# Binary cross-entropy on one core: two 64 KiB slots with float32 targets and even and odd partitions instead of three 56 KiB slots with bfloat16 targets

## The chip, the core and the metric

The kernel runs on one core of one Trainium2 chip. The metric is the device time of one execution in microseconds. Before the change the median of three runs is 1864.77 us (1864.36 to 1865.55). Data lie in the chip's main memory (HBM). A core has a working memory, SBUF, of 128 partitions; 16 DMA engines move data between the two. DVE (VectorE) and ACT (ScalarE) compute; POOL (GpSimd), SP (SyncE) and ACT each have a queue from which transfers are started.

## The reference

Two float32 arrays of 8192 x 8192 come in, `pred` and `target`; a target is 0 or 1. One array of the same shape goes out:

```
eps = 1e-7
pred = np.clip(pred, eps, 1 - eps)
return -(target * np.log(pred) + (1 - target) * np.log(1 - pred))
```

Each array has 268.4 MB, so at least 536.9 MB are read and 268.4 MB written. As a target is 0 or 1, the result is -log|p + t - 1|, and this is what the kernel computes.

## The kernel before

The arrays are seen flat. A chunk is a stretch of the flat array, laid out as 128 rows, one for each partition, of w columns of float32; a chunk's row is contiguous in HBM. Per partition there are 524288 columns in all. `plan` cuts them into 40 chunks: two of 5120 columns (`FIRST`), 35 of 14336 (`BIG`), two of 5632 (`LAST`; called a and b) and one of 1024 (`TAIL`; c).

Two buffers stay for the whole run. `ring_p` holds predictions, and results in their place: three slots of 56 KiB per partition, filled in turn, and a place for c. `ring_t` has a single slot for targets in bfloat16, and a place for c. The transfer casts the targets from float32 on their way.

A chunk goes through five steps, all in place on `ring_p`: DVE clips (`clip`, L88), DVE adds target minus one (`log`, L94, the only reader of `ring_t`), ACT takes the absolute value (L97) and the logarithm (L98), DVE negates (`back`, L102). A big chunk does its steps in two halves of 7168 columns.

The order on each engine is the order in which the program is written (`manual_schedule`), and an engine waits at an instruction until what it needs is there. Nearly all transfers go through POOL's queue: `load_t` (L75), `load_p` (L72) and `store` (L79). ACT's queue starts only the load of prediction 0, in two transfers, one of the even and one of the odd partitions; SP's queue starts the stores of a, b and c (L79, and `store_rows`, L84).

In the loop over the big chunks POOL starts, for chunk k, the load of target k+1, the store of chunk k and the load of prediction k+2. The target load waits for L94 of chunk k, as there is one slot; the store waits for L102 of chunk k; the prediction load goes into the slot of chunk k-1, whose store was started one round before.

Of the kernel before, what the change touches and what calls it, by code (L numbers as in the profile page):

```python
# [1 line left out]

# [4 lines left out]

EPS = 1e-7

BIG = 14 * 1024  # L10
FIRST = 5 * 1024
LAST = 5632
TAIL = 1024
SLOTS = 3


def plan(total):
    n = (total - 2 * FIRST - 2 * LAST - TAIL) // BIG
    assert n > 4 and total == 2 * FIRST + n * BIG + 2 * LAST + TAIL
    spots = [(FIRST, 0, 0), (FIRST, FIRST, FIRST)]  # L20
    spots += [(BIG, k % SLOTS * BIG, 0) for k in range(1, n + 1)]
    end = (n + 1) % SLOTS * BIG
    spots += [(LAST, end, 0), (LAST, end + LAST, LAST)]
    return spots + [(TAIL, SLOTS * BIG, BIG)]


@with_exitstack
def kernel(
    ctx: ExitStack,
    tc: tile.TileContext,  # L30
    pred: bass.AP,
    target: bass.AP,
    out: bass.AP,
):
    nc = tc.nc
    fp32 = mybir.dt.float32
    bf16 = mybir.dt.bfloat16
    Alu = mybir.AluOpType
    Act = mybir.ActivationFunctionType
    P = nc.NUM_PARTITIONS  # L40

    R, C = pred.shape
    spots = plan(R * C // P)
    n = len(spots)
    widths = [s[0] for s in spots]
    cols = [sum(widths[:k]) for k in range(n)]

    def chunk(ap, k):
        flat = ap.rearrange("r c -> (r c)")
        return flat[cols[k] * P : (cols[k] + widths[k]) * P].rearrange("(p w) -> p w", p=P)  # L50

    pool = ctx.enter_context(tc.tile_pool(name="rings", bufs=1))
    ring_p = pool.tile([P, SLOTS * BIG + TAIL], fp32, name="ring_p", tag="ring_p")
    ring_t = pool.tile([P, BIG + TAIL], bf16, name="ring_t", tag="ring_t")
    warm = pool.tile([1, 8], fp32, name="warm", tag="warm")

    def spot(k, part=(0, 1)):
        w, c, _ = spots[k]
        i, m = part
        return ring_p[:, c + i * w // m : c + (i + 1) * w // m]  # L60

    def spot_t(k, part=(0, 1)):
        w, _, c = spots[k]
        i, m = part
        return ring_t[:, c + i * w // m : c + (i + 1) * w // m]

    def load_p(k):
        if k == 0:
            for rows in (slice(0, P, 2), slice(1, P, 2)):
                nc.scalar.dma_start(out=spot(0)[rows], in_=chunk(pred, 0)[rows])  # L70
        else:
            nc.gpsimd.dma_start(out=spot(k), in_=chunk(pred, k))  # L72

    def load_t(k):
        nc.gpsimd.dma_start(out=spot_t(k), in_=chunk(target, k))  # L75

    def store(k):
        queue = nc.sync if k >= n - 3 else nc.gpsimd
        queue.dma_start(out=chunk(out, k), in_=spot(k))  # L79

    def store_rows(k):
        src, dst = spot(k), chunk(out, k)
        for first, last in ((0, 108), (108, 120), (120, 128)):
            nc.sync.dma_start(out=dst[first:last], in_=src[first:last])  # L84

    def clip(k, *part):
        p = spot(k, *part)
        nc.vector.tensor_scalar(  # L88
            out=p, in0=p, scalar1=EPS, scalar2=1 - EPS, op0=Alu.max, op1=Alu.min
        )  # L90

    def log(k, *part):
        p = spot(k, *part)
        nc.vector.scalar_tensor_tensor(  # L94
            out=p, in0=spot_t(k, *part), scalar=1.0, in1=p, op0=Alu.subtract, op1=Alu.add
        )
        nc.scalar.activation(out=p, in_=p, func=Act.Abs)  # L97
        nc.scalar.activation(out=p, in_=p, func=Act.Ln)  # L98

    def back(k, *part):  # L100
        p = spot(k, *part)
        nc.vector.tensor_scalar(out=p, in0=p, scalar1=-1.0, scalar2=None, op0=Alu.mult)  # L102

    with tc.manual_schedule():
        nc.vector.memset(warm, 1.0)  # L105
        load_t(0)
        load_p(0)
        load_t(1)
        load_p(1)
        load_p(2)  # L110
        nc.scalar.activation(out=warm, in_=warm, func=Act.Ln)  # L111
        for k in (0, 1):
            clip(k)
            log(k)
        load_t(2)
        back(0)
        store(0)
        back(1)
        store(1)
        load_p(3)  # L120
        a, b, c = range(n - 3, n)
        for k in range(2, n - 3):
            for h in (0, 1):
                clip(k, (h, 2))
                log(k, (h, 2))
            if k < n - 4:
                load_t(k + 1)
            else:
                load_t(a)
                load_t(b)  # L130
                load_p(c)
                load_t(c)
                back(k, (0, 2))
                for j in (a, b):
                    clip(j)
            if k < n - 4:
                back(k, (0, 2))
            back(k, (1, 2))
            store(k)
            if k + 2 < n - 3:  # L140
                load_p(k + 2)
            elif k + 2 == n - 3:
                load_p(a)
                load_p(b)
        log(a, (0, 2))
        log(a, (1, 2))
        clip(c)
        log(b, (0, 2))
        back(a, (0, 2))
        log(b, (1, 2))  # L150
        back(a, (1, 2))
        store(a)
        log(c)
        back(b, (0, 2))
        back(b, (1, 2))
        store(b)
        back(c)
        store_rows(c)


# [1 line left out]
_INS = ['pred', 'target']  # L162
_OUTS = [((8192, 8192), 'float32')]


# [23 lines left out]
```

## Time and profile before

| | |
|---|---|
| median of three runs | 1864.77 us |
| span of the profiled execution, first to last instruction | 1863.3 us |
| time of the profiled execution beside its span | not listed on its own; the median of the runs is 1.5 us above the span |
| DVE busy | 1121.6 us (60%) |
| ACT busy | 902.4 us (48%) |
| POOL busy, nearly all of it starting transfers | 178.7 us (10%) |
| HBM read and written | 536.87 and 268.44 MB, 432 GB/s over the span |
| DMA packets in POOL's queue | 16704 |

The page gives the busy time of each engine, 40 slices of the span with the busy share of the engines and of the 16 DMA engines in tenths (9 is 90% or more), the DMA queues, and the chain of work that ended last. A group of instructions is one line of the program on one engine, with its shapes, its count, its busy time in us, the mean duration in ns, and the idle time of the engine before these instructions with what ended it. In the order of time a row gives start, duration, engine, line and operation; what stands in brackets is the idle time before it and what ended it. The trace also has a record of every DMA packet (start, duration, size), and the times at which each of the 16 engines reported its share of a transfer.

### The profile page before, as it was taken

What the parts mean: (1) busy time and instruction counts of PE and PEld (TensorE: products, weight loads), DVE (VectorE), ACT (ScalarE), POOL (GpSimd) and SP (SyncE); (2) the same over time, 40 slices, a digit from 0 to 9 for tenths busy, and PEclk for the clock granted to TensorE, in tenths of its full rate; (3) what the DMA queues carried; (4) which work ended last, traced back from release to release, by engine and by line L of the source; (5) the groups of instructions that cost most, each with busy time, mean ns of one, the idle gap of its engine ahead of it and who ended that gap; (6) DMA issues with size and microseconds to landing.
All of it is one profiled execution on the core that took longest, in us unless ns stands there. A gap on an engine that the chain in (4) does not pass through costs nothing.

```text
span 1863.3 us, 713 instructions
## 1 busy us (share of the span) xinstructions
DVE 1121.6 (60%) x230; ACT 902.4 (48%) x156; POOL 178.7 (10%) x120
## 2 busy tenths in 40 slices
DVE  4666555555666566655555666566655555666565
ACT  4454444455555544444445555544444445555554
POOL 1111101111110011101111110011101111110020
DMA  9999999999999999999999999999999999999999
GB/s 344 348 370 356 355 356 355 355 355 355 357 375 374 374 372 355 355 355 355 355 355 355 359 374 374 375 375 361 355 355 356 356 356 355 356 367 374 374 353 352
DMA packets 17318, 671.15 MB, mean 360 GB/s; under 512 B 1952, under 2 KB 1952, under 8 KB 2336
## 3 DMA queue, kind: packets, MB, share of 16 engines
q0 software_dynamic: 16704, 662.18, 99.0%
q1 hardware_dynamic: 448, 6.29, 0.8%
q10 hardware_dynamic: 160, 2.62, 0.4%
q14 instruction: 6, 0.05, 0.0%
HBM read 536.87 MB, written 268.44 MB: 432 GB/s over the span
## 4 chain that ended last, share of the span: by engine, by line
DMA 60%; issue 35%; ACT 3%; DVE 1%; POOL 0%; POOLq 0%; DVEq 0%; PEldq 0%
DMA ring_t<-in_target_dram 58%; DMA ring_p<-in_pred_dram 2%; ACT ring_p L98 1%; ACT ring_p L97 1%; DVE ring_p L94 1%; DVE ring_p L102 0%; POOL out_dram L79 0%; DVE ring_p L88 0%; POOL ring_t L75 0%; POOLq L75 0%; POOL ring_p L72 0%; POOLq L79 0%; DVEq L94 0%; PEldq L184 0%
## 5 line engine op out<-in xcount | busy, mean ns | idle before, releaser
L97 ACT ACTIVATE ring_p<-ring_p 128x7168 f32<-128x7168 f32 (+3 forms) x77 | 452.0, 5870 | 940.7 <-DVE ring_p L94 940.7
L94 DVE SCALAR_TENSOR_TENSOR ring_p<-ring_t,ring_p 128x7168 f32<-128x7168 bf16 (+3 forms) x77 | 558.2, 7251 | 372.0 <-DMA ring_t<-in_target_dram 370.7
L102 DVE TENSOR_SCALAR ring_p<-ring_p 128x7168 f32<-128x7168 f32 (+3 forms) x77 | 285.4, 3707 | 329.4 <-ACT ring_p L98 329.4
L98 ACT ACTIVATE ring_p<-ring_p 128x7168 f32<-128x7168 f32 (+3 forms) x77 | 452.6, 5877 | 2.4
L88 DVE TENSOR_SCALAR ring_p<-ring_p 128x7168 f32<-128x7168 f32 (+3 forms) x75 | 284.6, 3794 | 24.4 <-DMA ring_p<-in_pred_dram 24.4
L79 POOL DMA_DIRECT2D out_dram<-ring_p x37 | 128.0, 3459 | 584.4 <-DVE ring_p L102 584.2
L75 POOL DMA_DIRECT2D ring_t<-in_target_dram x40 | 29.0, 724 | 1057.2 <-DVE ring_p L94 1056.4
L72 POOL DMA_DIRECT2D ring_p<-in_pred_dram x39 | 21.8, 561 | 2.5 <-issue 2.5
L111 ACT ACT_TABLE_LOAD x1 | 1.3, 1283 | 1.9 <-issue 1.9
L105 DVE MEMSET warm<- 1x8 f32 x1 | 0.1, 65 | 0.8 <-PEq L173 0.8
L111 ACT ACTIVATE warm<-warm 1x8 f32<-1x8 f32 x1 | 0.2, 208 | 0.0
L173 POOL MEMSET const-float32-0.0<- 128x1 f32 x1 | 0.1, 99 | 0.2 <-issue 0.2
L173 POOL MEMSET const-bfloat16-1.0<- 128x1 bf16 x1 | 0.1, 102 | 0.0
L173 POOL MEMSET const-uint8-127<- 128x1 uint8 x1 | 0.1, 100 | 0.0
L173 POOL MEMSET const-float32-1.0<- 128x1 f32 x1 | 0.1, 99 | 0.0
## 6 DMA issues: line engine op xcount, KB each, us to landing
ring_p<-in_pred_dram POOLq DMA_DIRECT2D x35, 7168.0 KB, 44.3
out_dram<-ring_p POOLq DMA_DIRECT2D x35, 7168.0 KB, 31.1
ring_t<-in_target_dram POOLq DMA_DIRECT2D x35, 3584.0 KB, 31.3
ring_p<-in_pred_dram POOLq DMA_DIRECT2D x2, 2816.0 KB, 37.1
out_dram<-ring_p SPq DMA_DIRECT2D x2, 2816.0 KB, 14.6
out_dram<-ring_p POOLq DMA_DIRECT2D x2, 2560.0 KB, 27.9
ring_t<-in_target_dram POOLq DMA_DIRECT2D x2, 1408.0 KB, 26.5
ring_p<-in_pred_dram ACTq DMA_DIRECT2D x2, 1280.0 KB, 10.5
```

The lines of the kernel that those rows point to most:

```text
L72: nc.gpsimd.dma_start(out=spot(k), in_=chunk(pred, k))
L75: nc.gpsimd.dma_start(out=spot_t(k), in_=chunk(target, k))
L79: queue.dma_start(out=chunk(out, k), in_=spot(k))
L88: nc.vector.tensor_scalar(out=p, in0=p, scalar1=EPS, scalar2=1 - EPS, op0=Alu.max, op1=Alu.min)
L94: nc.vector.scalar_tensor_tensor(out=p, in0=spot_t(k, *part), scalar=1.0, in1=p, op0=Alu.subtract, op1=Alu.add)
L97: nc.scalar.activation(out=p, in_=p, func=Act.Abs)
L98: nc.scalar.activation(out=p, in_=p, func=Act.Ln)
L102: nc.vector.tensor_scalar(out=p, in0=p, scalar1=-1.0, scalar2=None, op0=Alu.mult)
L105: nc.vector.memset(warm, 1.0)
L111: nc.scalar.activation(out=warm, in_=warm, func=Act.Ln)
L173: nc = _bacc.Bacc("TRN2", target_bir_lowering=False, num_devices=1)
```

## The change

Chunks, slots, types, split and order change together:

- `BIG` becomes 16384 columns, so that a row of a big chunk has 64 KiB; there are two slots for predictions and results instead of three. `FIRST` becomes 3584 and `LAST` 4096 columns; there are 31 big chunks instead of 35.
- `ring_t` holds float32, so target loads no longer cast.
- Stores and prediction loads of the big chunks are made in two transfers, of the even and of the odd partitions, as are the stores of the two first chunks and the prediction loads of a and b. Target loads stay whole. All stay on POOL's queue, but for the load of prediction 0 (ACT) and the stores of a, b and c (SP), as before. The store of the last big chunk is whole.
- Prediction k+1 now goes into the slot of chunk k-1, and each half of its load waits for the same half of that chunk's store. In the loop POOL starts both halves of store k-1, both halves of prediction load k+1, and target load k+1. The target load waits for the subtractions of chunk k.
- Steps of a big chunk are done in four pieces of 4096 columns instead of two of 7168: DVE's order in a round is four subtractions, four negations, four clips of the next chunk. In the last big chunk, the clips of a and b stand between the negations.

```diff
-BIG = 14 * 1024
-FIRST = 5 * 1024
-LAST = 5632
+BIG = 16 * 1024
+FIRST = 3584
+LAST = 4096
 TAIL = 1024
-SLOTS = 3
+SLOTS = 2
+PIECES = 4
...
-    ring_t = pool.tile([P, BIG + TAIL], bf16, name="ring_t", tag="ring_t")
+    ring_t = pool.tile([P, BIG + TAIL], fp32, name="ring_t", tag="ring_t")
...
+    even, odd = slice(0, P, 2), slice(1, P, 2)
+    every = slice(0, P)
+    bulk = nc.gpsimd
+
+    def load_p(k, rows=every, queue=bulk):
+        queue.dma_start(out=spot(k)[rows], in_=chunk(pred, k)[rows])
...
-    def store(k):
-        queue = nc.sync if k >= n - 3 else nc.gpsimd
-        queue.dma_start(out=chunk(out, k), in_=spot(k))
+    def store(k, rows=every, queue=bulk):
+        queue.dma_start(out=chunk(out, k)[rows], in_=spot(k)[rows])
...
         load_t(2)
-        back(0)
-        store(0)
-        back(1)
-        store(1)
-        load_p(3)
+        for k in (0, 1):
+            back(k)
+        for rows in (even, odd):
+            for k in (0, 1):
+                store(k, rows)
         a, b, c = range(n - 3, n)
-        for k in range(2, n - 3):
-            for h in (0, 1):
-                clip(k, (h, 2))
-                log(k, (h, 2))
-            if k < n - 4:
-                load_t(k + 1)
-            else:
-                load_t(a)
-                load_t(b)
+        m = PIECES
+        for i in range(m):
+            clip(2, (i, m))
+        for k in range(2, a):
+            last = k == a - 1
+            if k > 2:
+                for rows in (even, odd):
+                    store(k - 1, rows)
+            if not last:
+                for rows in (even, odd):
+                    load_p(k + 1, rows)
+            if last:
                 load_p(c)
                 load_t(c)
-                back(k, (0, 2))
+                for rows in (even, odd):
+                    for j in (a, b):
+                        load_p(j, rows)
+            for i in range(m):
+                log(k, (i, m))
+            if last:
                 for j in (a, b):
-                    clip(j)
-            if k < n - 4:
-                back(k, (0, 2))
-            back(k, (1, 2))
-            store(k)
-            if k + 2 < n - 3:
-                load_p(k + 2)
-            elif k + 2 == n - 3:
-                load_p(a)
-                load_p(b)
+                    load_t(j)
+            else:
+                load_t(k + 1)
+            for i in range(m):
+                back(k, (i, m))
+                if last and i in (1, 2):
+                    clip(a + i - 1)
+            if not last:
+                for i in range(m):
+                    clip(k + 1, (i, m))
+        store(a - 1)
+        clip(c)
...
-        clip(c)
         log(b, (0, 2))
         back(a, (0, 2))
         log(b, (1, 2))
         back(a, (1, 2))
-        store(a)
+        store(a, queue=nc.sync)
         log(c)
...
-        store(b)
+        store(b, queue=nc.sync)
```

## The prediction

> **What bounds the kernel now.** I read the page's slices first, then its queues, then the chain and the groups, and last the order of time of one chunk.
>
> ```profile
> DVE 1121.6 (60%) x230; ACT 902.4 (48%) x156; POOL 178.7 (10%) x120
> DMA  9999999999999999999999999999999999999999
> q0 software_dynamic: 16704, 662.18, 99.0%
> DMA 60%; issue 35%; ACT 3%; DVE 1%; POOL 0%; POOLq 0%; DVEq 0%; PEldq 0%
> L94 DVE SCALAR_TENSOR_TENSOR ring_p<-ring_t,ring_p 128x7168 f32<-128x7168 bf16 (+3 forms) x77 | 558.2, 7251 | 372.0 <-DMA ring_t<-in_target_dram 370.7
> ```
>
> The 16 DMA engines are in the top tenth in all 40 slices, and POOL's queue (q0) alone holds them for 99.0% of the span. DVE waits 370.7 us for targets, so the engines are fed by the transfers and not the other way round; the chain, which hops from target load to target load, says the same.
>
> ```profile
> 1652.20 0.53 POOL L75 DMA_DIRECT2D ring_t<-in_target_dram  x1 [29.43 <-DVE ring_p L94]
> 1668.98 3.89 DVE L88 TENSOR_SCALAR ring_p<-ring_p 128x7168 f32<-128x7168 f32 x1
> 1669.36 3.63 POOL L79 DMA_DIRECT2D out_dram<-ring_p  x1 [16.63 <-DVE ring_p L102]
> 1672.98 0.53 POOL L72 DMA_DIRECT2D ring_p<-in_pred_dram  x1
> 1683.60 7.62 DVE L94 SCALAR_TENSOR_TENSOR ring_p<-ring_t,ring_p 128x7168 f32<-128x7168 bf16 x1 [10.73 <-DMA ring_t<-in_target_dram]
> 1702.98 0.53 POOL L75 DMA_DIRECT2D ring_t<-in_target_dram  x1 [29.47 <-DVE ring_p L94]
> ```
>
> One chunk of 14336 columns (a column is one float32 on 128 partitions). From the target load at 129.28 to that at 1753.73 there are 32 periods: 50.76 us each, 3.541 ns a column. A period reads 7.34 MB of predictions and 7.34 MB of targets and writes 7.34 MB: 434 GB/s. The page's 360 GB/s counts targets as they arrive, in two bytes. A load issue takes POOL 0.53 us, but 3.63 us where it begins inside a clip on DVE: POOL is held until the clip ends.
>
> The trace's packet records give the limit. On each engine one packet is one partition's row, and the next begins 2113 ns later for 57344 B, 833 ns for 22528 B, 155 ns for 4096 B: 27.2 B/ns plus 4.8 ns a packet. A target packet (57344 B read, 28672 B written in bfloat16) begins 2112 ns after the last: the read side sets its time, and the cast saves none. From 2.85 to 1859.7 us there is no moment in which the engines run dry.
>
> The sum of before: 524288 columns x 3.541 ns = 1856.5 us; 2.1 us pass before the first packet, 1.3 us after the last one (1861.96), and 3.4 us are slow packets at the start and the lag of one engine, which lands its share of a transfer 1.0 us behind the first engine at 45 us and 3.0 us behind from 500 us on. Together 1863.3, the profiled span. The median of the runs is 1864.77, so 1.5 us lie around the span.
>
> **The change part by part.**
> *Float32 targets, 64 KiB rows.* The same bytes are read and written in HBM. A chunk is now 16384 columns; 24 packets per engine at 65536/27.2 + 4.8 = 2414 ns are 57.94 us. Today 24 packets at 2113 ns are 50.71 of the 50.76 us, so three handovers between transfers cost 0.05 us, 0.017 each; five handovers (both halves of store and prediction load, and the target) cost 0.09. 31 chunks x 58.03 = 1798.9 against 35 x 50.76 = 1776.7; the small pieces lose 6144 columns, x 3 x 4 B x 8 rows / 27.2 = 21.7 us. The transfers together change by 1798.9 - 1776.7 - 21.7 = +0.5 us. Fewer packets and more handovers cancel.
>
> *Two slots instead of three.* A prediction load now waits for the store of the chunk two before it, which today it does not. Count from the landing of target k (0), on the engine that is last. The queue then holds store k-1: even half to 9.7 us (4 packets of 2.414), odd half to 19.3; then prediction k+1, even to 29.0, odd to 38.6, and target k+1 to 58.0. Each must be issued before the queue is dry:
> - Even load: its store half lands at 9.7 + 0.3 (at 63 us a last packet ended 0.3 us before its landing). From issue to first packet ACT's first load took 1.3 us (0.74 to 2.07); POOL's first took at most 4.6 (1.24 to 5.82, behind ACT's packets). First data at 11.3 to 14.6, needed at 19.3. DVE is then in the subtractions, beside which no issue of POOL is seen; if they hold it as the clip did, 3.6 us more, up to 18.2. Still covered, by 1.1 to 8 us; I take no hold and 1.3.
> - Behind this wait on POOL stand the odd load and the target load. The odd one is free at 19.6, may be held 2.3 us by a negation (4096 columns between the 1.62 us of 2816 and the 3.10 of 5632), and has data by 26.5; needed at 29.0. The target needs the four subtractions: 4 x 4.42 us (4096 columns between 3.09 at 2816 and 5.49 at 5120) = 17.7; needed at 38.6.
> - Store k needs the last negation: 4.42 + 4 pieces x 2 x 3.61 on ACT (between 2.55 at 2816 and 4.47 at 5120) + 2.29 = 35.6; needed at 58.0. Clips of k+1 end at 38.9 + 4 x 2.29 = 48.1; needed at 58.0.
>
> So nothing per chunk. A float32 second operand of the subtraction isn't in the trace: between 4.42 us (as bfloat16) and twice that. Even doubled, the four end at 35.4, store k is ready near 45, and DVE is busy 54 of 58 us; I take 4.42, since this operation runs at 1.04 ns a column where one-input ones run at 0.52, so it isn't fed by the width of one operand.
>
> *Start.* 15.7 MB are queued before the first wait, to 38.3 us. Prediction 1 lands near 19.6, target 2 can be issued at about 28. The four half stores of chunks 0 and 1 run from 57.6 to 66.0; the even load of chunk 3 is free at 62.1, with data at 63.4 to 66.7, or 70.3 if held: 0 to 4 us once. I take 0.
>
> *End.* Count from the landing of target 32: store 31 to 19.3, chunk c to 21.7, predictions a, b to 31.4, their targets to 41.1. Store 32 waits for negations between which stand the clips of a and b, each waiting for its odd half: a's at 29.3, then clip, negation, clip, negation, 4 x 2.29 = 38.5; data at 39.8 to 43.1, needed at 41.1. 0 to 2 us once; I take 0. After that the stores of 32, a, b, c are issued well before the queue ends, as today.
>
> Sum: 1863.3 + 0.5 = 1863.8, and with the 1.5 around it 1865.3 us.
>
> **Rivals.**
> - *The refill runs dry* (the other side: slower). If the even load's data come later than 9.7 us after its store half ends, every chunk idles by the excess, about 30 times. For it: a landing, a wait and an issue of POOL now lie in the loop. Against: 1.1 to 8 us of margin. At 0.3 us past the margin 1865 + 10 = 1875; at 2 us, 1925. 0.09. [...]
> - *Rows in step.* At 59 us the last packets of a target load took 2280 to 3064 ns instead of 2131, on all 16 engines together; 55 such packets are in the records, most in the first 420 us, until the engines have drifted apart. Rows 64 KiB apart may collide anew in each transfer: one round of 0.5 us in each of 5 x 31 transfers is +78, 1943 us. Against: 4 KiB rows run at the fitted 155 ns, and 0.4% of the packets are slow today. 0.07. [...]
> - *Half transfers don't use all engines from POOL's queue.* Stores and prediction loads, two thirds of 1856 us, would double: 3100 us. Against: ACT's two 64-row loads, with target 0 beside them, moved 5.24 MB between 2.07 and 14.96 us, 407 GB/s with the start-up in it. 0.03.
> - *A 65536 B row goes as two packets*, so that the change doesn't do what it says: 744 x 4.8 ns = +3.6, 1868.9 us. 0.04.
> - *A gap at start or end*: +1 to +6, 1868 in the middle. 0.04.
> - *Faster*: lag (2 to 3 us) and slow start vanish: 1861.5 at best, as the bytes alone take 805.3 MB/435.2 = 1850.4 us. 0.03.
>
> **How the numbers follow.** The forecast, covered refills, has 0.70. 0.2% is 3.7 us, about what can be told from no change. Same: 0.70 + half of the gaps 0.02 = 0.72. Slower: 0.09 + 0.07 + 0.03 + 0.04 + 0.02 = 0.25. Faster: 0.03, if the last case reaches past 1861. The range 1861 to 1875 holds the forecast (its own range 1863 to 1868), the split row, the gaps, the faster case and a refill that is barely late, some 0.82.
>
> **What would show it.** Right: the slices stay full, chunk period 58.0 us, packets of 65536 B at 2414 ns, waits of POOL on its store halves without a dry queue. Wrong: slices below the top tenth at the turn from stores to loads; packets longer than 2.42 us; 32768 B packets; subtractions of 8.8 us. The weakest point is that POOL's 64-row transfers are taken to run like its 128-row ones.

## The result and the profile after

The changed kernel takes 1870.92 us (median of five runs, 1870.84 to 1873.84) against 1864.77: 1.0036 times the time before, 95% interval 1.0026 to 1.0047. It is 6 us slower. The prediction was 1865.3 us, in a range from 1861 to 1875.

These are lines of the page of the changed kernel; they answer to the lines of before.

```profile
span 1869.2 us, 1058 instructions
DVE 1131.1 (61%) x392; ACT 917.9 (49%) x264; POOL 152.1 (8%) x172
DMA  9999999999999999999999999999999999999999
q0 software_dynamic: 16000, 798.76, 99.0%
L93 DVE SCALAR_TENSOR_TENSOR ring_p<-ring_t,ring_p 128x4096 f32<-128x4096 f32 (+2 forms) x131 | 558.4, 4323 | 323.4 <-DMA ring_t<-in_target_dram 323.3
L72 POOL DMA_DIRECT2D ring_p<-in_pred_dram x67 | 91.3, 1363 | 1223.0 <-DMA out_dram<-ring_p 1223.0
```

The span is 5.9 us longer. The DMA engines are still in the top tenth everywhere, and DVE still waits for targets (323.3 us). New is the last line: POOL now waits 1223.0 us for stores to land, at the issue of prediction loads. The share of busy time can't show what this costs: a packet that takes longer counts as busy all the while, and q0 holds the engines for 99.0% of the span in both kernels.

One chunk of the changed kernel in the order of time:

```profile
168.06 17.43 DVE L93 SCALAR_TENSOR_TENSOR ring_p<-ring_t,ring_p 128x4096 f32<-128x4096 f32 x4 [10.85 <-DMA ring_t<-in_target_dram]
177.99 0.53 POOL L72 DMA_DIRECT2D ring_p<-in_pred_dram  x1 [31.51 <-DMA out_dram<-ring_p]
185.40 4.49 DVE L101 TENSOR_SCALAR ring_p<-ring_p 128x4096 f32<-128x4096 f32 x2
187.64 2.36 POOL L72 DMA_DIRECT2D ring_p<-in_pred_dram  x1 [9.13 <-DMA out_dram<-ring_p]
190.00 0.53 POOL L75 DMA_DIRECT2D ring_t<-in_target_dram  x1
203.87 1.06 POOL L78 DMA_DIRECT2D out_dram<-ring_p  x2 [13.34 <-DVE ring_p L101]
```

The even load is issued at 177.99, 9.9 us after the target landed, while DVE subtracts: 0.53 us, so subtractions do not hold POOL. The odd one falls into two negations and takes 2.36 us. From the target at 168.06 to that of the last big chunk at 1796.15 there are 28 periods, 58.15 us on average.

The packet records tell where the time went. A 65536 B row is one packet, and the next begins 2414 ns later, as worked out. The difference lies in packets that take longer than the median of their size (counted here where they take at least 0.1 us longer). Summed over all packets and divided by 16 engines, that excess was 1.9 us before and is 6.8 us now. Between 50 and 1800 us nearly all of it before (1.0 us) and most of it now (4.6 of 5.5 us) stands in one place: the eighth and last packet of a target load and the first packet of the store behind it, that is, where the engines turn from reading targets to writing results. Most of the rest are first packets of prediction loads, at 68 and 601 us. Before, the excess dies out: after 500 us only 0.13 us are added until 1800 us, and the times at which the engines finish a transfer stand in a fixed pattern (at 852, 1055 and 1258 us the first eight are 0, 0.01, 0.05, 0.06, 0.16, 0.24, 0.25 and 0.28 us apart from the first). After the change the pattern is disturbed again and again (the last engine lands 3.2 us behind the first at 427 us, 4.8 at 591, 4.1 at 1443 and 4.7 at 1578), and 2.8 us are added between 500 and 1800 us. Near the end the engines run dry from 1834.3 to 1836.1 us, 1.0 us on average. So +4.9 us of slow packets and +1.2 us of dry time (0.15 us of it at 1818) come to 6.1 us; other terms, each of 0.5 us or less, bring this to the 5.9 us by which the span grew.

### The profile page after: what moved, and what is told of

Its sections match the earlier page's. It is cut to its first block, busy times and chain, and to the rows that moved or that the text cites. A ratio compares the mean times of both kernels' runs of the same rounds, so it can differ in the third digit from the quotient of the medians.

```text
span 1869.2 us, 1058 instructions
## 1 busy us (share of the span) xinstructions
DVE 1131.1 (61%) x392; ACT 917.9 (49%) x264; POOL 152.1 (8%) x172
## 3 DMA queue, kind: packets, MB, share of 16 engines
q10 hardware_dynamic: 160, 1.84, 0.3%
## 4 chain that ended last, share of the span: by engine, by line
DMA 58%; ACT 24%; issue 10%; DVE 7%; POOL 1%; DVEq 0%; POOLq 0%; PEldq 0%
DMA ring_t<-in_target_dram 31%; DMA out_dram<-ring_p 26%; ACT ring_p L97 12%; ACT ring_p L96 12%; DVE ring_p L93 5%; DVE ring_p L101 2%; POOL ring_p L72 1%; DMA ring_p<-in_pred_dram 1%; DVE ring_p L87 0%; POOL ring_t L75 0%; DVEq L93 0%; POOLq L75 0%; PEldq L193 0%; POOLq L78 0%
## 5 line engine op out<-in xcount | busy, mean ns | idle before, releaser
L96 ACT ACTIVATE ring_p<-ring_p 128x4096 f32<-128x4096 f32 (+2 forms) x131 | 462.0, 3527 | 930.5 <-DVE ring_p L93 930.5
L93 DVE SCALAR_TENSOR_TENSOR ring_p<-ring_t,ring_p 128x4096 f32<-128x4096 f32 (+2 forms) x131 | 558.4, 4323 | 323.4 <-DMA ring_t<-in_target_dram 323.3
L97 ACT ACTIVATE ring_p<-ring_p 128x4096 f32<-128x4096 f32 (+2 forms) x131 | 463.5, 3538 | 4.1
L101 DVE TENSOR_SCALAR ring_p<-ring_p 128x4096 f32<-128x4096 f32 (+2 forms) x131 | 291.0, 2242 | 281.9 <-ACT ring_p L97 281.9
L87 DVE TENSOR_SCALAR ring_p<-ring_p 128x4096 f32<-128x4096 f32 (+1 forms) x129 | 285.2, 2272 | 118.0 <-DMA ring_p<-in_pred_dram 110.3
L72 POOL DMA_DIRECT2D ring_p<-in_pred_dram x67 | 91.3, 1363 | 1223.0 <-DMA out_dram<-ring_p 1223.0
L78 POOL DMA_DIRECT2D out_dram<-ring_p x65 | 38.8, 602 | 427.6 <-DVE ring_p L101 424.2
L75 POOL DMA_DIRECT2D ring_t<-in_target_dram x36 | 21.8, 607 | 32.5 <-DVE ring_p L93 31.7
```

The source lines that it names most:

```text
L72: queue.dma_start(out=spot(k)[rows], in_=chunk(pred, k)[rows])
L75: bulk.dma_start(out=spot_t(k), in_=chunk(target, k))
L78: queue.dma_start(out=chunk(out, k)[rows], in_=spot(k)[rows])
L87: nc.vector.tensor_scalar(out=p, in0=p, scalar1=EPS, scalar2=1 - EPS, op0=Alu.max, op1=Alu.min)
L93: nc.vector.scalar_tensor_tensor(out=p, in0=spot_t(k, *part), scalar=1.0, in1=p, op0=Alu.subtract, op1=Alu.add)
```

## The experiments

The question is what keeps the turn from targets to stores expensive. Slow packets, in the table, are the excess defined above; the lag is the time from the first to the last engine's landing in one transfer near 1780 us. Times before are 1864.5 to 1865.3 us in each set of runs. Span, slow packets and lag are those of one profiled execution, which need not be a typical one: with bfloat16 targets and with targets in halves it was the slowest of its set (1878.56 and 1878.52 us), so their slow packets belong to those times and not to the medians.

| kernel | median us | ratio to before (95%) | span us | slow packets, all | 50 to 500 us | 500 to 1800 us | lag |
|---|---|---|---|---|---|---|---|
| before | 1864.77 | | 1863.3 | 1.9 | 0.9 | 0.1 | 3.0 |
| changed | 1870.92 | 1.0026 to 1.0047 | 1869.2 | 6.8 | 2.7 | 2.8 | 4.1 |
| changed, 56 KiB rows | 1873.56 | 1.0028 to 1.0054 | 1869.8 | 6.4 | 2.1 | 3.3 | 3.2 |
| changed, bfloat16 targets | 1872.32 | 1.0032 to 1.0057 | 1876.8 | 13.8 | 3.0 | 9.4 | 4.1 |
| changed, targets in halves too | 1872.64 | 1.0032 to 1.0058 | 1876.7 | 11.8 | 1.8 | 8.6 | 4.0 |
| changed, three slots of 56 KiB, bfloat16 | 1866.55 | 1.0003 to 1.0020 | 1865.5 | 2.3 | 1.2 | 0.1 | 3.7 |
| before, with halves | 1865.14 | 0.9994 to 1.0012 | 1863.4 | 1.9 | 1.2 | 0.1 | 3.5 |
| before, with halves and two slots | 1907.44 | 1.0199 to 1.0247 | 1903.3 | 31.0 | 4.5 | 24.1 | 3.3 |
| changed, a negation moved | 1870.65 | 1.0019 to 1.0039 | 1869.0 | 5.3 | 3.6 | 0.4 | 5.0 |
| changed, a negation moved, both ends covered | 1870.86 | 1.0020 to 1.0043 | 1868.3 | 4.6 | 2.2 | 1.1 | 4.8 |
| changed, in quarters | 1873.34 | 1.0031 to 1.0059 | 1870.4 | 4.7 | 2.1 | 1.4 | 6.8 |

### Rows of 56 KiB, and bfloat16 targets

The first theory was the rival "rows in step": 64 KiB rows make the engines collide. The second was the type. Each was undone alone.

```diff
-BIG = 16 * 1024
-FIRST = 3584
-LAST = 4096
+BIG = 14 * 1024
+FIRST = 5 * 1024
+LAST = 5632
```

> The changed kernel with the chunk sizes of before (14336 columns, 56 KiB rows; first 5120, last 5632); slots, types, halves and order as changed. Slow packets cost the changed kernel 6.8 us of each engine on average, 1.9 us before; they stand at the turn from a target load to a store. If the 64 KiB rows cause the surplus, slow packets fall to about 2 us here and the time to 1866.5 us (1864.8, 1.2 for 70 more handovers at 0.017, about 1 for a gap at the end). If order, halves or type cause it, they stay at 6 to 7 us and the time is 1871 to 1872 us.

```diff
-    ring_t = pool.tile([P, BIG + TAIL], fp32, name="ring_t", tag="ring_t")
+    ring_t = pool.tile([P, BIG + TAIL], mybir.dt.bfloat16, name="ring_t", tag="ring_t")
```

> The changed kernel with bfloat16 targets again. If float32 targets cause the surplus of slow packets, slow packets fall to about 2 us and the time to 1866 us. If rows, halves or order cause it: 1871 us, slow packets 6 to 7 us. The subtraction should keep its 4.32 us a piece and the packet pitch its 2.41 us in either case.

Neither brought the time back (1873.56 and 1872.32 us), and slow packets were 6.4 and 13.8 us, the second more than either case had expected. Neither the row size nor the type alone is the cause. Only at the first turn, near 57 us and ahead of any refill, is there a difference that goes with the chunk sizes: 1.0 to 1.3 us of slow packets in the kernels with 64 KiB rows, 0.5 to 0.8 us in those with 56 KiB. The kernels with the surplus also scatter: the 56 KiB run gave 1869.8 to 1875.1 us where the kernel before keeps within 1 us in the same set.

### Whole transfers, and other halves

Both edits concern the halves: one takes them away in POOL's queue, the other makes them of neighbouring partitions. The line with `for rows` changes in all four loops of POOL's queue; one is shown.

```diff
-        for rows in (even, odd):
+        for rows in (every,):
```

> The changed kernel with whole stores and whole prediction loads in POOL's queue. With nothing queued behind a store, the prediction load starts only after the store has landed: about 0.3 us to the landing, 0.5 to issue, 1.3 to 4.6 to the first packet, so 2 to 5 us dry per chunk, 30 times: 1930 to 2020 us, if the halves are what covers the refill. If POOL's queue has other cover, 1870 us. Handovers save 1 us in either case.

```diff
+    lower, upper = slice(0, P // 2), slice(P // 2, P)
...
-        for rows in (even, odd):
+        for rows in (lower, upper):
```

> The changed kernel with halves of the partitions 0 to 63 and 64 to 127 instead of even and odd ones. If which partitions a transfer touches doesn't matter, 1871 us. If a half of neighbouring partitions reaches only half of the paths into the partitions' memory, stores and prediction loads run at half their rate: two thirds of 1856 us again, 3100 us.

Whole transfers: 2050.4 us. The page's slices show the dry stretches, and POOL's order of time shows a period of 965.75 - 902.09 = 63.7 us (64.1 on average over the loop) in place of 58.15.

```profile
DMA  9998999899999998999989999999899989989899
```

```profile
902.09 2.02 POOL L72 DMA_DIRECT2D ring_p<-in_pred_dram  x1 [47.68 <-DMA out_dram<-ring_p]
965.75 2.39 POOL L72 DMA_DIRECT2D ring_p<-in_pred_dram  x1 [47.25 <-DMA out_dram<-ring_p]
```

So with two slots the halves cover the refill, and their cover is worth 180 us; it was expected at 60 to 150. The packet records give 132 us of dry time, about 4.4 us a chunk and so within the 2 to 5 us expected, although POOL's issue falls into negations here (2.0 and 2.4 us). What was left out are the slow packets: 57 us in place of 6.8, of which 20 us are the first packets after the dry stretches, and nearly all the rest are at the turns. Halves bring no rate of their own, as the kernel before with halves will show (1865.14 us against 1864.77, see below); here they serve as two completion points, and the run shows what that is worth.

Neighbouring partitions: 3032.5 us in a single execution, against 3100 expected. The page's slices still say busy everywhere; the line to read is the rate.

```profile
DMA  9999999999999999999999999999999999999998
DMA packets 16616, 805.38 MB, mean 266 GB/s; under 512 B 2784, under 2 KB 2784, under 8 KB 3168
```

266 GB/s instead of 431; half of the 65536 B packets took 4.64 us or more instead of 2.42. The median time from issue to landing is 40.8 us for prediction loads of the big chunks and 77.0 us for their stores, against 19.0 and 32.5 us in the changed kernel. The time fits the case of half the paths, but no record shows the paths. Even and odd partitions are thus the right halves here, and POOL's 64-row transfers of them keep the rate of a 128-row one: from 1094.87 to 1152.86 us of the changed kernel the first engine lands each of the four halves 9.64 to 9.68 us after the transfer ahead of it, and the target load 19.35 us after. This is the point that the prediction called its weakest.

### Where the turn is

Two theories for the turn: rows of a 128-row transfer meet rows of a 64-row one, or any turn costs as long as the engines' offsets don't settle.

```diff
     def load_t(k):
-        bulk.dma_start(out=spot_t(k), in_=chunk(target, k))
+        for rows in (even, odd) if widths[k] == BIG else (every,):
+            bulk.dma_start(out=spot_t(k)[rows], in_=chunk(target, k)[rows])
```

> The changed kernel with target loads of big chunks in even and odd halves too, so that every big transfer on the queue is a half. If the slow packets come from the change between 128-row and 64-row transfers (a row of the one and a row of the other meeting at the turn), they fall to about 2 us and the time to 1866 us. If any turn from loads to stores brings them once the engines' offsets don't settle, they stay at 5 to 8 us, and the time is 1871 to 1874 us, 0.5 of it for 31 more handovers.

1872.64 us (1868.75 to 1878.52), slow packets 11.8 us, more than the 5 to 8 expected, and at the turn now in the last packet of the odd half. So the turn is slow without the mixture too.

### Halves without two slots, and two slots without the new order

Now one part alone, put into the kernel before. The first edit gives it the halves, the second also two slots; nothing else changes.

```diff
     def load_p(k):
...
-            nc.gpsimd.dma_start(out=spot(k), in_=chunk(pred, k))
+            big = widths[k] == BIG
+            for rows in (slice(0, P, 2), slice(1, P, 2)) if big else (slice(0, P),):
+                nc.gpsimd.dma_start(out=spot(k)[rows], in_=chunk(pred, k)[rows])
...
     def store(k):
...
-        queue.dma_start(out=chunk(out, k), in_=spot(k))
+        big = widths[k] == BIG
+        for rows in (slice(0, P, 2), slice(1, P, 2)) if big else (slice(0, P),):
+            queue.dma_start(out=chunk(out, k)[rows], in_=spot(k)[rows])
```

> The kernel before (three slots, 56 KiB rows, bfloat16 targets, its order) with one thing of the change: stores and prediction loads of big chunks in even and odd halves. If the halves cause the surplus of slow packets, these rise from 1.9 to 5 to 8 us per engine, the lag of the last engine keeps moving instead of settling at 3.0 us, and the time is 1870 to 1873 us. If the new order with two slots causes it, slow packets stay near 2 us and the time is 1866 us (70 more handovers at 0.017).

```diff
-SLOTS = 3
+SLOTS = 2
```

> The kernel before with halves and two slots of 56 KiB instead of three, its own order on DVE: the reverse of the three-slot run. If the refill behind a landing store brings the slow packets, they rise from 1.9 to 5 us or more per engine and the time to 1870 to 1873 us; if the order of the compute does, slow packets stay near 2 us and the time at 1865 us.

And the reverse, three slots in the changed kernel:

```diff
-BIG = 16 * 1024
-FIRST = 3584
-LAST = 4096
+BIG = 14 * 1024
+FIRST = 5 * 1024
+LAST = 5632
...
-SLOTS = 2
+SLOTS = 3
...
-    ring_t = pool.tile([P, BIG + TAIL], fp32, name="ring_t", tag="ring_t")
+    ring_t = pool.tile([P, BIG + TAIL], mybir.dt.bfloat16, name="ring_t", tag="ring_t")
```

> The changed kernel (halves, four pieces, its order on DVE) with three slots of 56 KiB and bfloat16 targets, so that a prediction load goes into a slot whose store ended a round earlier and POOL doesn't wait for a landing. Both 56 KiB rows with two slots and bfloat16 targets alone kept 6 to 14 us of slow packets. If the refill behind a landing store brings them, they fall to about 2 us, the lag settles near 3 us, and the time is 1865 to 1866.5 us. If the order of the compute or the four pieces bring them, they stay at 5 us or more and the time is 1870 to 1873 us.

Halves alone: 1865.14 us, slow packets 1.9 us. Halves and two slots: 1907.44 us, 31.0 us of slow packets, with dry stretches beside them (2.9 us at 74 us, 4.9 us at the end). Three slots in the changed kernel: 1866.55 us, 2.3 us. Slots are the only edit between the first two runs. POOL's longest waits in these two kernels (microseconds in total, times, longest), first the kernel before with halves and its three slots, then that with two:

```profile
POOL ring_t L77 <- DVE ring_p L98: 1021.6, 37, 32.8
POOL out_dram L83 <- DVE ring_p L106: 584.1, 36, 16.6
```

```profile
POOL ring_p L74 <- DMA out_dram<-ring_p: 864.9, 67, 28.7
POOL out_dram L83 <- DVE ring_p L106: 590.2, 36, 16.6
```

In the first, no wait of a prediction load for a store stands in the list; in the second it is the longest of POOL's. In the changed kernel the three slots bring 4.4 of the 6 us back; that run has 56 KiB rows and bfloat16 targets as well, which alone brought nothing. So the second slot's price comes with the prediction load that has to wait for a landing store: it brings the slow packets, and with them the time. The size was missed in the two-slot run: 1870 to 1873 us were expected, 1907 came. There the even load's issue also falls into a clip and takes up to 2.9 us, so that after 450 us it ends only 0.4 to 2.6 us before the first engine needs the rows, and the first packets of that load are slow as well.

### Is it the margin?

The margin is the time from the end of POOL's issue to the moment at which the first engine turns to that load. In the three-slot run it is 26 to 41 us in the loop, in the changed kernel about 4 us for the even and 1.8 to 2.6 us for the odd half after 450 us. The load waits for the last engine's share of the store: in the changed kernel the engines land the even half of a store from 175.06 to 177.70 us, and the even load is issued at 177.99 us. So the lag eats the margin of the engines that are ahead. Where the margin fell under 2 us, at 596 (1.84) and 1583 us (1.88), the load's first packets were slow on seven and three engines.

The kept packet records say this more broadly. They cover nine kernels that refill behind a store in even and odd halves, or in quarters (all two-slot kernels of the table, and the one with moved clips in the section on the end). For each round of the loop after 500 us, take the smallest margin among its prediction loads, and the slow packets from these loads through the next turn:

| smallest margin in the round | rounds | slow packets in a round, mean us | range |
|---|---|---|---|
| under 1.5 us | 21 | 1.26 | 0.7 to 1.9 |
| 1.5 to 2 us | 21 | 0.67 | 0.1 to 1.1 |
| 2 to 2.5 us | 74 | 0.10 | 0 to 0.4 |
| over 2.5 us | 87 | 0.05 | 0 to 0.6 |

Half of the 42 rounds under 2 us are of the kernel before with two slots, the other half of five changed kernels. Slow packets thus go with a margin under 2 us. In the changed kernel the lag had risen ahead of both such rounds, from 4.1 to 4.7 us at 572 and at 1559 us, and stood at 4.5 us after them. This also tells why the profiles with bfloat16 targets and with targets in halves have so many: eight and seven of their rounds lie under 2 us and hold 8.0 of 9.5 and 6.8 of 8.7 us. In the changed kernel it is two rounds with 1.4 of 2.8 us.

The first edit lifts the odd half's margin: DVE takes the first negation between its second and third subtraction.

```diff
             for i in range(m):
                 log(k, (i, m))
+                if i == 1:
+                    back(k, (0, m))
...
-            for i in range(m):
+            for i in range(1, m):
                 back(k, (i, m))
```

> The changed kernel with one step moved on DVE: the first negation of a big chunk stands between its second and third subtraction, so that POOL's issue of the odd prediction load no longer falls into the first two negations, which hold it to 2.4 us. In the changed kernel that issue ends 2.0 to 2.5 us before the first engine needs its rows, and the load's first packets are slow where it is under 2 us. If this margin is what disturbs the engines, it rises by about 1.9 us to 4, slow packets fall from 6.8 towards 2 to 4 us, and the time to 1866 to 1868 us. If any refill behind a landing disturbs them, whatever the margin, slow packets stay at 6 to 8 us and the time at 1871 us.

```profile
1167.80 0.53 POOL L72 DMA_DIRECT2D ring_p<-in_pred_dram  x1 [31.04 <-DMA out_dram<-ring_p]
1171.86 8.75 DVE L93 SCALAR_TENSOR_TENSOR ring_p<-ring_t,ring_p 128x4096 f32<-128x4096 f32 x2
1177.43 0.54 POOL L72 DMA_DIRECT2D ring_p<-in_pred_dram  x1 [9.11 <-DMA out_dram<-ring_p]
```

The odd issue, at 1177.43, now lies in the subtractions and takes 0.54 us; after 100 us both margins are 3.4 us or more. After 720 us the offsets settle, and from 500 to 1800 us slow packets add 0.4 us instead of 2.8. Together with the table this says that the thin margin disturbed the engines in that stretch. It does not say that the margin is what the 6 us hang on, for the time is 1870.65 us: 1866 to 1868 was missed. 3.6 us of slow packets fell between 50 and 500 us, the lag settled at 5.0 us instead of 3.0, and the engines ran dry for 2.1 us on average near the end. Against the profile of the changed kernel, 1.5 us less of slow packets and 1.1 us more of dry time nearly cancel.

Two more edits went for a larger margin, one by quarters, one by more work behind the first refill, together with the end:

```diff
+    quarters = [slice(i, P, 4) for i in range(4)]
...
-        for rows in (even, odd):
+        for rows in quarters:
```

> The changed kernel with stores and prediction loads of big chunks in four quarters (partitions 0, 4, 8 and on; 1, 5, 9; and so forth) instead of two halves: behind a landed quarter three quarters, 14.5 us, are still queued instead of 9.7. If the margin is what disturbs the engines, it rises to 6 us or more, the lag settles as before, slow packets fall to 2 to 3 us, and the time to 1866 to 1867.5 us, 1 to 2 us of it for 124 more handovers. If any refill behind a landing disturbs them, slow packets stay at 6 us or more and the time is 1872 us.

```diff
         a, b, c = range(n - 3, n)
+        load_p(c)
+        load_t(c)
...
-                load_p(c)
-                load_t(c)
...
-                if last and i in (1, 2):
-                    clip(a + i - 1)
...
         store(a - 1)
+        clip(a)
+        clip(b)
         clip(c)
```

> The run with the moved negation, and the two thin places at start and end covered: both loads of c (2.4 us) queued behind the first four stores, so that the first refill (chunk 3) has 2.4 us more cover, and the clips of a and b behind the last negation. In the run with the moved negation the first refill came too late, its first packets were slow on 14 engines (0.5 us), and the next turn from targets to stores was slow on all 16 (1.2 us). If late refills cause what is left, slow packets fall from 5.3 to 3 to 3.5 us, and the time from 1870.7 to about 1868.5 us. If two slots cost something beyond late refills, slow packets stay at 5 us and the time at 1870 to 1871 us.

Quarters: 1873.34 us (1.0031 to 1.0059 of before), slow packets 4.7 us, of which 1.4 between 500 and 1800 us; the margin is mostly 5 us or more, the lag settles at 6.3 and then 6.8 us, and the engines run dry for 4.1 us on average near the end. Covered ends: 1870.86 us (1.0020 to 1.0043), slow packets 4.6 us. The first refill adds only 0.1 us of slow packets now, but near the end 2.5 us are dry, 1.4 of them where the loads of c stood before, between the last store in halves and the loads of a and b. Both miss: three edits raised the margin above 2 us, and none of them shortened the kernel. Between this run's profile (span 1868.3 us) and that of the three-slot run (1865.5) the slow packets differ by 2.2 us, most of the difference. Why two slots start with more slow packets, and settle with a larger lag, stays open.

### The end

```diff
-                if last and i in (1, 2):
-                    clip(a + i - 1)
...
         store(a - 1)
+        clip(a)
+        clip(b)
         clip(c)
```

> The changed kernel with the clips of a and b behind the last negation of the last big chunk. Its store is then issued about 4 us earlier than at 1834.9 us and the dry stretch from 1834.3 to 1836.1 us (1.0 us of each engine on average) goes: minus 1 us, 1870 us, if the engines' mean counts; no change, 1871 us, if the lagging engine alone sets the end, since that engine had work until 1836 us.

The order of time around the last big store, first the changed kernel, then this one:

```profile
1834.88 0.54 POOL L78 DMA_DIRECT2D out_dram<-ring_p  x1 [15.23 <-DVE ring_p L101]
```

```profile
1831.84 2.02 POOL L78 DMA_DIRECT2D out_dram<-ring_p  x1 [12.30 <-DVE ring_p L101]
```

The store is issued 3.0 us earlier and the dry stretch is gone but for 0.1 us, yet the time is 1873.16 us (1.0030 to 1.0055), no shorter. The executions scatter from 1870.2 to 1876.0 us, more than the 1 us in question, so the records have to decide. The dry stretch only let the first engines wait for the last: with it, the lag fell from 3.3 to 1.6 us; without it, a lag of 3.7 to 5.2 us stands until the last store, and from 1863.8 us on the engines are dry for 2.7 us on average, where the changed kernel has 0.4. The lagging engine sets the end.

## Why the prediction was right or wrong

- *What bounds the kernel*: right. Transfers on 16 full engines, before and after.
- *Float32 targets, 64 KiB rows*: right. 2414 ns a packet, one packet a row, no gain and no loss from rows or cast beyond the scatter (each undone alone). A handover costs less than the 0.017 us worked out: in undisturbed rounds the period is 58.00 us, in the changed kernel (from 1063 to 1527 us) as in the run with the moved negation, against 58.03.
- *Two slots: "nothing per chunk"*: this step failed. The times in it were right: subtractions at 4.42 us a piece of 4096 columns, as taken (the 4323 ns of the page's group mix in smaller pieces), no hold beside them, an issue of the odd load of 2.4 us in all where a hold of 2.3 us on top was allowed for, and no dry queue in the loop. Wrong was the conclusion that a load which comes before the queue is dry costs nothing: the mean period is 58.15 us, and single rounds take up to 58.9. The sum followed one engine and so left out the lag of the last engine, 3 to 5 us, by which the margin of the first engine shrinks. Rounds with a margin under 2 us have slow packets at the turn. That accounts for about half of those between 500 and 1800 us; for those before 500 us the cause stays open.
- *"beside which no issue of POOL is seen"*: this reading of the trace was wrong. The trace of before has one issue beside subtractions, and it takes 0.54 us, so "no hold" could have been read instead of chosen:

```profile
1822.07 6.09 DVE L94 SCALAR_TENSOR_TENSOR ring_p<-ring_t,ring_p 128x2816 f32<-128x2816 bf16 x2
1822.44 0.54 POOL L79 DMA_DIRECT2D out_dram<-ring_p  x1 [10.32 <-DVE ring_p L102]
```

- *Start*: 0 to 4 us once, taken as 0. The first refill's packets were slow on ten engines, 0.4 us on average.
- *End*: 0 to 2 us once, taken as 0. The engines ran dry for 1.0 us on average, but the run with the moved clips shows that the time doesn't hang on it.
- *The rivals*: "the refill runs dry" came nearest, though the queue did not run dry in the loop; its point of decision was put at no margin, while slow packets set in under some 2 us of margin. "Rows in step" had the right packets in view, which the records of before show at 59 us, and the wrong cause: row size, which shows at the first turn alone, with about 0.5 us. "Half transfers don't use all engines" put the time at 3100 us, near the 3032.5 us of neighbouring partitions, but the slices there show the engines busy throughout, so what it says of the engines was not shown.
- *The numbers*: 1865.3 was 5.6 us low; the measured time lies in the range, on the slower side, to which 0.25 was given. That it lies in the range is luck in part: the forecast's own range ended at 1868, and the upper part was there for a split row, a gap at the ends and a refill that runs dry, of which only a gap near the end came, 1.2 us of dry time on average. The missed term is the slow packets, +4.9 us, taken as 0 in the sum.

## What to carry to other kernels

A transfer that is issued before the queue runs dry is not yet free: count the margin on the engine that is furthest ahead, after a landing that waits for the engine furthest behind, and keep it above the 2 us under which packets became slow in these runs. More margin than that made the packets steadier but did not shorten this kernel. A third buffer that takes the landing out of the loop was worth more here than longer rows and fewer chunks. If a buffer must be refilled behind its own store, split it into halves of even and odd partitions: that is 180 us of 2050 here, while halves of neighbouring partitions cost 1160.

## What the runs showed of the hardware that was not expected

- With all 16 DMA engines full, the last packet of a target load in front of a store can take longer: at 56 us of the changed kernel, with the engines within 0.7 us of each other, on all 16 and by up to 1.5 us. In the kernel before, this excess falls from 0.53 us at 59 us to 0.01 at 412 us while the lag of the last engine grows from 1.0 to 2.9 us; from 852 to 1258 us the offsets of the first eight engines then hold to 0.02 us. That the engines push each other apart is an inference.
- POOL's issue of a transfer takes 0.53 us beside a two-input subtraction on DVE. It takes up to 3.63 us where it begins inside a one-input clip of 7168 columns (before), and up to 2.45 us inside negations of 4096 columns (changed).
- After a dry stretch, all 16 engines restart nearly together (lags of 0.4 to 1.1 us in the run with whole transfers), and both the packets after the restart and the next turn are slow: 57 us of slow packets in that run.
